# The down products of both feed-forward layers by a seven-product scheme of halves

## The chip, the cores and the metric

The kernel runs on one core of one Trainium2 chip. The metric is device time in microseconds (us) of one execution. A core has TensorE (PE in the profile; PEld is its loading of weights), VectorE (DVE), ScalarE (ACT), GpSimd (POOL) and SyncE (SP), which here only issues DMAs. The engines run their own instruction streams in order and wait for each other by semaphores.

## The reference, cut to what matters

A two-layer trunk over 1024 tokens of width 1024. Layer 0 is a gated mixer, layer 1 an attention over chunks; behind each stands a SwiGLU block, and only that block is changed:

```python
def _swiglu_ffn(x, g_norm, w_gate_up, w_down):     # x: 1024 x 1024
    h = _rms_norm(x, g_norm)
    gate, up = jnp.split(h @ w_gate_up, 2, axis=-1)  # each 1024 x 2816
    return (jax.nn.silu(gate) * up) @ w_down         # w_down: 2816 x 1024
```

Everything is float32, and results have to agree closely with float32.

## The kernel before, in words

All activations stand transposed: features on the 128 partitions, 1024 tokens along the free side. The residual stream x is eight tiles of 128x1024. A float32 number is carried as two parts, hi and lo (`split`, L116: ACT rounds to hi by a copy, DVE takes lo = source - hi), and a product is three matmuls: hi·hi, hi·lo, lo·hi. Every matmul in question is 128x128 weights by 128x512 columns.

A feed-forward block (`ffn`, from L591) has two phases.

*Gate and up*, f = 0 to 21 (a tile of 128 hidden features each, L706). The pair (gate tile f, up tile f) by the pair (token half 1, token half 2) is a 2x2 product of halves, and already done with seven products instead of eight (the Winograd form). Its operands are A (weights; sums S1 to S4 made by POOL, `quad_sum12` and `quad_sum34`) and B (activations; sums T1 to T4 made once). In the steady loop the order on PE is A11·B11, S2·T2, S1·T1, A12·B21, S3·T3, S4·B22, A22·T4, each 12 matmuls, 84 in all. Between them DVE and ACT add up the products, scale by the norm, apply silu (`gate`, L634) and multiply (`up`, L638) into yy, which is stored to memory (`yd`, L755). The weights of f+1 are prepared meanwhile: two loads (`wraw`), four POOL sums, splits of S1|S2, A11|A12, S3|S4 and A22 into four pairs of buffers `whi`, `wlo`, each free once f's product has used it.

*Down*, from L760: 22 K tiles y(f), loaded again from `yd` and split (`load_y`), each with a weight tile `wd` (`prep_w`, L93). Two K tiles at a time, `rows_all` and `mm_rows` (L220) make 8 output tiles times 2 token halves: six matmuls into a PSUM bank, then one DVE addition into x (L230). The last pair of layer 0 goes through `rows_late`, and the last four K tiles of layer 1 too, interleaved with the final norm.

Places in SBUF are few: 28 slots (`slot`) hold B in the first phase and y in the second; eight places (`xplace`) hold x, which in the first phase stands in memory (`xd`), while the places serve as ac, bu, gg and yy of two iterations in turn; three scratch tiles (`scratch`, tag scr) rotate.

The order written in the program is a priority. A planner of the framework, with its own costs, places instructions on each engine's queue and may put a later one that is ready ahead of an earlier one that is not; a new tile waits for all users of the one whose place it takes. All DMAs of these phases are issued by SP, in the planned order.

Of the kernel before, what the change touches and what calls it, by code (L numbers as in the profile page):

```python
# [15 lines left out]
P = 128  # L16
# [33 lines left out]
class Trunk:  # L50
# [492 lines left out]
    QUAD = ("S12", "S34", "A", "AA")  # L543

    def b_plain(self, B, i, xe, xo, ge, go):
# [45 lines left out]
    def ffn(self, x, layer, sqp):  # L591
        nc, a = self.nc, self.a
        with ExitStack() as st:
            psum = self.ps8 if layer == 0 else self.pool(st, "psF", 8, psum=True)
            dp = self.pool(st, f"fdram{layer}", 1, dram=True)
            xd = dp.tile([KT, P, S], F32, name="xd")
            yd = dp.tile([FT, P, S], F32, name="yd")
            self.ffn_slots(st, layer)
            acc = self.const.tile([P, S], F32, name="rbc")
# [3 lines left out]

            def xplace(d, name):
                if layer == 0:
                    return sqp.tile([P, S], F32, name=name, tag=f"x{d}")
                return self.hp.tile([P, S], F32, name=name, tag=f"hhi{d}")

# [21 lines left out]
            def outs(f):  # L630

                return [xplace(4 * (f % 2) + j, f"{n}{f}") for j, n in enumerate(("ac", "bu", "gg", "yy"))]

# [70 lines left out]
            q = qn  # L704
            wl = [(a[f"wd{layer}"][f], None) for f in range(FT)]
            for f in range(2, FT):  # L706
# [43 lines left out]
                up(o, 1, None)  # L750
                self.quad_s34(qn) if more else self.prep_w()
# [3 lines left out]
                nc.sync.dma_start(yd[f], yy)  # L755
                self.quad_a22(qn) if more else self.prep_w()
                q = qn
# [3 lines left out]

            def load_y(f):
                j = 16 + 6 * (f // 2 % 2) + 3 * (f % 2)
# [7 lines left out]
            x = []  # L771
            for d in range(KT):
                x.append(xplace(d, f"x{layer}_{d}"))
                nc.sync.dma_start(x[d], xd[d])
            xt[:] = x
            n = FT if layer == 0 else FT - 4
            for f in range(0, n, 2):
                ws2 = [self.take_w(), self.take_w()]
                ys = [yt.pop(f), yt.pop(f + 1)]
                if layer == 0 and f == FT - 2:  # L780
                    self.rows_late(psum, ws2, ys, x)
                else:
                    self.rows_all(psum, "ps", ws2, ys, x)
                self.prep_w()
                self.prep_w()
                for k in (f + 4, f + 5):
                    if k < FT:
                        load_y(k)
            if layer == 0:
                return x  # L790

            ws4 = [self.take_w() for _ in range(4)]
            ys = [yt.pop(FT - 4 + i) for i in range(4)]
            parts = [slice(0, 512), slice(512, 768), slice(768, 1024)]
            accs, xgs = {}, {}

            def done(d, t):
# [4 lines left out]
                if d < 2:  # L804
                    accs[k] = self.slot(8 + len(accs), f"facc{len(accs)}", F32)[:, 0:w]
                self.square_add(self.hx, accs[k], x[d][:, t], d < 2, eng)
                for c in range(t.start, t.stop, 256):
                    k = (c, d // 4)
                    if d % 4 == 0:
                        xgs[k] = self.slot(len(xgs), f"xg{len(xgs)}", F32).rearrange("p (k t) -> p k t", k=4)  # L810
                    nc.scalar.activation(xgs[k][:, d % 4, :], x[d][:, c:c + 256], AF.Copy,
# [22 lines left out]

            self.rows_late(psum, ws4, ys, x, (parts[0],), done)
            running = [finish(parts[0])]
            for t in parts[1:]:
                for d in range(KT):
                    self.mm_rows(psum, "ps", ws4, ys, x, d, t)
                    done(d, t)  # L840
                    if d in (2, 6):
                        next(running[-1])
# [252 lines left out]
def prepare(i):  # L1095
# [23 lines left out]
    for l in range(2):  # L1119
        gu = i["ffn_w_gate_up"][l]  # L1120
        o[f"wg{l}"] = cols2(gu[:, :FF])
        o[f"wup{l}"] = cols2(gu[:, FF:])
        o[f"wd{l}"] = rows(i["ffn_w_down"][l])
    o["wk"] = cols(i["w_kv"][:, :D])
# [33 lines left out]
```

## Time and profile before

| | |
|---|---|
| median of 3 runs | 2527.73 us (2523.31 to 2528.09) |
| profiled execution | 2528.11 us, its span 2526.3 us |
| granted TensorE clock | 0.995 |
| busy: PE, PEld, DVE | 2466.4, 2041.4, 1710.3 us |
| busy: ACT, POOL | 920.1, 361.8 us |
| DMA | 241.08 MB |
| gate and up, layer 0 and 1 (steady) | about 682 to 1006 and 1942 to 2266 us |
| down, layer 0 and 1 | about 1006 to 1230 and 2266 to 2511 us |

Times in the trace count from the first instruction. "idle before <-releaser" is the time an engine stood still ahead of an instruction and what ended it. Matmuls overlap in the pipeline, so the length of one in the profile is more than the distance from one to the next.

### The profile page before, as it was taken

The page shows a single profiled execution, that of the slowest core. Times are in us where ns is not written, and L with a number is a line of the kernel's source. Part 1 is how long each engine was busy: PE and PEld are TensorE (multiplying, and loading weights), DVE is VectorE, ACT ScalarE, POOL GpSimd, SP SyncE. Part 2 cuts the span into 40 slices and gives each one's busy share as a digit, 9 for nine tenths or more (in the row PEclk, how much of TensorE's full clock was granted, in tenths as well). Part 3 has the DMA queues.
Part 4 walks back from the last instruction along what each step waited for, and adds up shares of the span by engine and source line. Part 5 has one row for each costly group of instructions (what it writes and reads, how often), then busy time and mean ns, then how long its engine had stood idle before and what let it go on. Part 6 is the DMA issues. An engine that isn't in the chain of part 4 may idle for free.

```text
span 2526.3 us, 30361 instructions
## 1 busy us (share of the span) xinstructions
PE 2466.4 (98%) x11646; PEld 2041.4 (81%) x11646; DVE 1710.3 (68%) x2713; ACT 920.1 (36%) x1445; POOL 361.8 (14%) x285
## 2 busy tenths in 40 slices
PE   8999999999999999999999999999999999999997
PEld 6888888887788888888877888877877888888887
DVE  6227677678666566767877777777777656667665
ACT  5123232236333333111445555554453323331113
POOL 3001111121222321000210100000112222210001
PEclk9999999999999999999999999999999999999999
DMA  6223222223222224322322222243322222253222
GB/s 201 83 96 97 67 71 63 67 100 109 92 84 89 79 84 168 141 100 84 127 56 65 65 61 61 66 140 96 128 89 97 79 92 76 83 187 132 91 82 67
DMA packets 94737, 241.08 MB, mean 95 GB/s; under 512 B 8704, under 2 KB 37376, under 8 KB 94592
## 3 DMA queue, kind: packets, MB, share of 16 engines
q1 hardware_dynamic: 92288, 234.95, 28.3%
q10 hardware_dynamic: 2304, 4.20, 0.5%
q8 instruction: 91, 1.49, 0.2%
q14 instruction: 54, 0.44, 0.1%
HBM read 178.29 MB, written 52.43 MB: 91 GB/s over the span
## 4 chain that ended last, share of the span: by engine, by line
PE 86%; DVE 8%; ACT 2%; DMA 2%; issue 1%; POOL 1%; DVEq 0%; SPq 0%; ACTq 0%; POOLq 0%
PE ps L588 29%; PE ps L229 23%; PE pj L215 8%; PE ps L215 7%; PE pj L229 3%; PE po L1005 2%; PE ps L333 2%; PE ps L335 2%; PE ps L334 2%; PE pt L978 2%; PE ps L456 1%; PE s L955 1%; PE s L958 1%; DVE x L459 1%; DVE wlo L118 1%
## 5 line engine op out<-in xcount | busy, mean ns | idle before, releaser
L117 ACT CAST whi<-wraw 128x1024 fp32r<-128x1024 f32 (+1 forms) x213 | 202.1, 962 | 567.4 <-PE ps L229 431.9
L230 DVE TENSOR_TENSOR x<-x,ps 128x512 f32<-128x512 f32 (+1 forms) x432 | 281.4, 674 | 167.4 <-PE ps L229 166.8
L118 DVE TENSOR_TENSOR wlo<-wraw,whi 128x1024 fp32r<-128x1024 f32 (+1 forms) x213 | 235.8, 1117 | 59.4 <-ACT whi L117 59.4
L118 DVE TENSOR_TENSOR wlo<-s,whi 128x1024 fp32r<-128x1024 f32 x84 | 106.7, 1270 | 150.4 <-ACT whi L117 146.0
L117 ACT CAST whi<-s 128x1024 fp32r<-128x1024 f32 x84 | 88.0, 1050 | 320.9 <-POOL s L518 207.5
L517 POOL TENSOR_TENSOR s<-wraw 128x512 f32<-128x512 f32 x42 | 54.5, 1298 | 827.1 <-DMA wraw<-wup 775.8
L588 PE MATMUL ps<-b1h,whi 128*128 128x512 f32 x368 | 144.9, 394 | 7.7 <-ACT whi L117 6.3
L215 PE MATMUL pj<-hhi,whi 128*128 128x512 f32 x368 | 151.3, 411 | 0.2 <-DVE x L459 0.2
L588 PE MATMUL ps<-b1h,wlo 128*128 128x512 f32 x368 | 144.9, 394 | 3.0 <-DVE wlo L118 2.7
L215 PE MATMUL pj<-hlo,whi 128*128 128x512 f32 x368 | 147.6, 401 | 0.0
L215 PE MATMUL pj<-hhi,wlo 128*128 128x512 f32 x368 | 146.6, 399 | 0.0
L588 PE MATMUL ps<-b2h,whi 128*128 128x512 f32 x368 | 143.6, 390 | 1.6 <-ACT ac L681 1.6
L588 PE MATMUL ps<-b1l,whi 128*128 128x512 f32 x368 | 144.4, 392 | 0.0
L588 PE MATMUL ps<-b2l,whi 128*128 128x512 f32 x368 | 143.2, 389 | 0.0
L588 PE MATMUL ps<-b2h,wlo 128*128 128x512 f32 x368 | 143.2, 389 | 0.0
L588 PE MATMUL ps<-bth,wlo 128*128 128x512 f32 x336 | 130.9, 389 | 0.5 <-DVE wlo L118 0.5
L105 POOL TENSOR_TENSOR wraw<-wraw,gv 128x1024 f32<-128x1024 f32 x24 | 48.8, 2038 | 572.4 <-DMA wraw<-wv_att 238.0
L588 PE MATMUL ps<-bth,whi 128*128 128x512 f32 x336 | 130.8, 389 | 0.0
L588 PE MATMUL ps<-btl,whi 128*128 128x512 f32 x336 | 130.7, 389 | 0.0
L396 POOL TENSOR_TENSOR mt<-mt,bbc 128x256 f32<-128x256 f32 x64 | 60.8, 950 | 444.4 <-ACT mt L395 441.5
L967 ACT ACTIVATE p<-p,mn 128x640 f32<-128x640 f32 (+4 forms) x128 | 89.3, 698 | 73.4 <-DVE mn L962 72.1
L117 ACT CAST thi<-pt 128x640 fp32r<-128x640 f32 (+4 forms) x128 | 71.5, 559 | 101.1 <-PE pt L978 100.2
(474 smaller groups left out, 6555.8 us busy)
## 6 DMA issues: line engine op xcount, KB each, us to landing
wraw<-wg SPq DMA_DIRECT2D x44, 512.0 KB, 3.5
wraw<-wup SPq DMA_DIRECT2D x44, 512.0 KB, 3.6
yd<-yy SPq DMA_DIRECT2D x44, 512.0 KB, 3.5
wraw<-wd SPq DMA_DIRECT2D x44, 512.0 KB, 4.4
y<-yd SPq DMA_DIRECT2D x44, 512.0 KB, 5.3
vd<-vt SPq DMA_DIRECT2D x32, 256.0 KB, 2.6
wraw<-wu SPq DMA_DIRECT2D x16, 512.0 KB, 3.6
wraw<-wout SPq DMA_DIRECT2D x16, 512.0 KB, 3.6
```

What stands on the lines that cost most here:

```text
L117: self.nc.scalar.copy(hi, src)
L118: self.nc.vector.tensor_tensor(lo, src, hi.bitcast(F32), ALU.subtract)
L215: nc.tensor.matmul(ps[s], wt[:, c], ht[:, t], start=(kt == 0 and i == 0), stop=(kt == KT - 1 and i == 2),)
L229: nc.tensor.matmul(o, wt[:, c], yt[:, t], start=(j == 0 and i == 0), stop=(j == last and i == 2))
L230: nc.vector.tensor_tensor(x[d][:, t], x[d][:, t], o, ALU.add)
L333: nc.tensor.matmul(ps[tt], hhi[:, t], whi[:, c], start=(kt == 0), stop=False)
L334: nc.tensor.matmul(ps[tt], hhi[:, t], wlo[:, c], start=False, stop=False)
L335: nc.tensor.matmul(ps[tt], hlo[:, t], whi[:, c], start=False, stop=(kt == KT - 1))
L396: nc.gpsimd.tensor_tensor(t2, t2, _bc_mid(bbc[:, g * P:(g + 1) * P], 2), ALU.add)
L517: nc.gpsimd.tensor_tensor(s12[:, HALF[0]], u[:, HALF[0]], u[:, HALF[1]], ALU.add)
L588: nc.tensor.matmul(ps, w[:, c], h, start=(start and i == pairs[0] and n == 0), stop=(stop and i == pairs[-1] and n == 2), skip_group_check ...
L967: nc.scalar.activation(pt[:, 0:nc_], pt[:, 0:nc_], AF.Exp, bias=mn, scale=-1.0, accum_out=sm)
```

## The change

Of the 22 K tiles of each down product, 16 (f = 2 to 17) go through the same seven-product form: four groups g of four K tiles (two halves of two), each with four pairs of output tiles j and j+4. One such step, k = 4g + j, takes the place of 4 K tiles by 2 output tiles by 2 token halves.

Weights come in a new layout `wds`, 128 x (A11|A12|A21|A22) of 256 columns. `down_load` loads a step's tile and a second copy of A22, and POOL makes S1 to S4 in four subtractions or additions of 256 columns; `down_t1` and `down_t2` split 1024 and 768 columns.

The sums T1 to T4 of y are made during gate and up, for two K tiles at a time, by `y_parts`: five pieces of DVE and ACT work, put into the loop by calls of `some()`, three in the next (even) f and two in the one after. Hi and lo parts go to memory (`td`) in seven stores of 512 KB for two K tiles; `load_t` brings them back, 14 tiles for a group. K tiles 0, 1 and 18 to 21 keep the old path. The places of ac, bu and gg are no longer taken in turn, yy goes round three places, and x comes back in another order.

```diff
+    def down_load(self, layer, k):
+        src = self.a[f"wds{layer}"][k]
+        r1 = self.wp.tile([P, 1024], F32, name="wraw", bufs=2)
+        nc.sync.dma_start(r1, src)
+        r2 = self.scratch(f"r2_{k}")
+        nc.sync.dma_start(r2[:, 512:768], src[:, 768:1024])
+        a11, a12, a21, a22 = (r1[:, c:c + 256] for c in (0, 256, 512, 768))
+        TT = nc.gpsimd.tensor_tensor
+        TT(r2[:, 0:256], a11, a21, ALU.subtract)
+        TT(a21, a21, r2[:, 512:768], ALU.add)
+        TT(a22, a21, a11, ALU.subtract)
+        TT(r2[:, 256:512], a12, a22, ALU.subtract)
...
-                return [xplace(4 * (f % 2) + j, f"{n}{f}") for j, n in enumerate(("ac", "bu", "gg", "yy"))]
+                places = (0, 1, 4 if f == 1 else 6, (3, 5, 7)[f % 3])
+                return [xplace(j, f"{n}{f}") for j, n in zip(places, ("ac", "bu", "gg", "yy"))]
+            def y_parts(f):
+                p = (f - 2) // 2
+                ye, yo = ys.pop(f), ys.pop(f + 1)
+                t = self.scratch(f"ty{f}")
+                def out(n, y, place):
+                    hi = xplace(place, f"yh{f}_{n}", F32R)
+                    nc.scalar.copy(hi, y)
+                    lo = y.bitcast(F32R)
+                    TT(lo, y, hi.bitcast(F32), sub)
+                    nc.sync.dma_start(td[p, 2 * n], hi.bitcast(F32))
+                    nc.sync.dma_start(td[p, 2 * n + 1], y)
+                def t12():
+                    TT(t[:, t1], ye[:, t2], ye[:, t1], sub)
+                    TT(t[:, t2], yo[:, t2], t[:, t1], sub)
+                yield t12
+                def t34():
+                    TT(ye[:, t2], yo[:, t2], ye[:, t2], sub)
+                    t4 = xplace(4, f"yt{f}", F32R)
+                    r = t4[:, t2].bitcast(F32)
+                    TT(r, yo[:, t1], t[:, t2], sub)
+                    nc.scalar.copy(t4[:, t1], r)
+                    TT(t4[:, t2], r, t4[:, t1].bitcast(F32), sub)
+                    nc.sync.dma_start(td[p, 6], t4.bitcast(F32))
+                yield t34
+                yield lambda: out(1, yo, 2)
+                yield lambda: out(0, ye, 4)
+                yield lambda: out(2, t, 2)
...
                 self.quad_s12(qn) if more else self.prep_w()
+                some()
                 prod(pa, "A12", "B21")
...
                 self.quad_a(qn) if more else self.prep_w()
+                some()
                 prod(pb, "S3", "T3")
...
+                    d0 = self.down_load(layer, 0)
+                    self.down_t1(d0)
+                some()
                 prod(pb, "A22", "T4", stop=True)
...
+                if f < FT - 4:
+                    ys[f] = yy
+                    if f % 2:
+                        todo += y_parts(f - 1)
+                else:
+                    nc.sync.dma_start(yd[f], yy)
...
-            for f in range(4):
-                load_y(f)
+            load_y(0, 16)
+            load_y(1, 19)
+            order = (2, 4, 5, 7, 6, 0, 1, 3)
+            for d in order:
+                x[d] = xplace(d, f"x{layer}_{d}")
                 nc.sync.dma_start(x[d], xd[d])
...
+            def load_t(g):
+                for n in (0, 4, 2, 6):
+                    for i in range(2):
+                        t = []
+                        for e in range(1 if n == 6 else 2):
+                            t.append(self.slot(14 * (g % 2) + 2 * (n + e) + i, f"t{g}_{n + e}_{i}"))
+                            nc.sync.dma_start(t[-1].bitcast(F32), td[2 * g + i, n + e])
...
+                        yield
+            for _ in load_t(0):
+                pass
+            ws2 = [self.take_w(), self.take_w()]
+            y2 = [yt.pop(0), yt.pop(1)]
+            d1 = self.down_load(layer, 1)
+            for d in order:
+                for s in range(2):
+                    self.mm_rows(psum, "ps", ws2, y2, x, d, HALF[s])
+            def dprod(q, bank_, A, key, into, start=False, stop=False):
+                ahi, alo = q[A]
+                for i in range(2):
+                    c = slice(i * P, (i + 1) * P)
+                    bhi, blo = T[q["g"], key, i]
+                    for n, (w, h) in enumerate(((ahi, bhi), (ahi, blo), (alo, bhi))):
+                        nc.tensor.matmul(q[bank_], w[:, c], h, ...)
+                for d, s in into:
+                    o = x[q["j"] + 4 * d][:, HALF[s]]
+                    TT(o, o, q[bank_], add)
+            for k in range(nq + 1):
+                if k < nq:
+                    qn["B"], qn["C"], qn["A"] = bank(), bank(), bank()
+                q3 = self.down_load(layer, k + 2) if k + 2 < nq else None
+                if q:
+                    dprod(q, "B", "S3", "T3", [(1, 1)])
+                if k < nq:
+                    dprod(qn, "B", "A11", "B11", [(0, 0)], True)
+                    if k:
+                        self.down_t2(qn)
...
+                if q:
+                    dprod(q, "C", "S4", "B22", [(0, 1)], stop=True)
+                if k < nq:
+                    dprod(qn, "C", "S1", "T1", [(1, 1)], True)
+                    dprod(qn, "B", "S2", "T2", [(0, 1)])
+                    if q2:
+                        self.down_t1(q2)
...
+                if q:
+                    dprod(q, "B", "A22", "T4", [(1, 0)], stop=True)
+                if k < nq:
+                    dprod(qn, "A", "A12", "B21", [(0, 0)], True, True)
+                    if g + 1 < ng:
+                        if k % 4 == 0:
+                            loads = load_t(g + 1)
+                        for _ in range(2 + (k % 4 == 0)):
+                            next(loads, None)
+                    else:
+                        f = FT - 4 + k % 4
+                        load_y(f, 3 * (k % 4))
+                q, qn, q2 = qn, q2, q3
```

## Rows read from the trace of the kernel before

**Rows 1.** The page: PE's busy time, and the shares of the ending chain.
```profile
PE 2466.4 (98%) x11646; PEld 2041.4 (81%) x11646; DVE 1710.3 (68%) x2713; ACT 920.1 (36%) x1445; POOL 361.8 (14%) x285
PE 86%; DVE 8%; ACT 2%; DMA 2%; issue 1%; POOL 1%; DVEq 0%; SPq 0%; ACTq 0%; POOLq 0%
```
**Rows 2.** The ending chain in order of time: start, length, what (gate/up, down).
```profile
662.60 343.52 PE ps L588 x1507
1006.12 217.60 PE ps L229 x960
...
1922.70 343.36 PE ps L588 x1507
2266.06 195.84 PE ps L229 x864
```
**Rows 3.** Windows: length; busy of PE, PEld, DVE, ACT, POOL; clock; DMA share; GB/s.
```profile
681.70:1005.80 324.10, 324.10 (x1432) 268.36 (x1431) 196.08 (x257) 105.01 (x139) 81.28 (x64) 1.00 0.28 97
1006.10:1223.70 217.60, 217.60 (x962) 180.18 (x961) 151.84 (x203) 39.09 (x41) 3.75 (x2) 1.00 0.30 105
```
**Rows 4.** DVE groups by line, gate and up of layer 0: busy, mean ns, idle.
```profile
L642 DVE TENSOR_TENSOR yy<-yy,gg 128x512 f32<-128x512 f32 x34 | 23.4, 688 | 0.6
L118 DVE TENSOR_TENSOR wlo<-wraw,whi 128x1024 fp32r<-128x1024 f32 x18 | 21.8, 1210 | 3.1 <-ACT whi L117 3.1
L118 DVE TENSOR_TENSOR wlo<-wraw,whi 128x512 fp32r<-128x512 f32 x17 | 11.5, 679 | 0.0
```
**Rows 5.** DVE and ACT groups by line, down of layer 0 (1050 to 1200).
```profile
L230 DVE TENSOR_TENSOR x<-x,ps 128x512 f32<-128x512 f32 x111 | 73.3, 685 | 46.4 <-PE ps L229 46.4
L118 DVE TENSOR_TENSOR wlo<-wraw,whi 128x1024 fp32r<-128x1024 f32 x14 | 16.5, 1219 | 0.0
...
L117 ACT CAST whi<-wraw 128x1024 fp32r<-128x1024 f32 x13 | 13.1, 1052 | 107.1 <-PE ps L229 107.1
```
**Rows 6.** DVE's order of time, end of f = 19 and most of f = 20.
```profile
969.03 0.68 DVE L118 TENSOR_TENSOR wlo<-wraw,whi 128x512 fp32r<-128x512 f32 x1
...
970.34 0.69 DVE L642 TENSOR_TENSOR yy<-yy,gg 128x512 f32<-128x512 f32 x1
973.58 0.69 DVE L720 TENSOR_TENSOR bu<-ps,ac 128x512 f32<-128x512 f32 x1 [2.55 <-PE ps L588]
978.19 1.34 DVE L118 TENSOR_TENSOR wlo<-s,whi 128x1024 fp32r<-128x1024 f32 x1 [3.91 <-ACT whi L117]
...
981.67 0.69 DVE L729 TENSOR_TENSOR bu<-ps,ac 128x512 f32<-128x512 f32 x1 [0.41 <-PE ps L588]
...
984.39 0.69 DVE L748 TENSOR_TENSOR gg<-ps,bu 128x512 f32<-128x512 f32 x1 [0.57 <-PE ps L588]
```
**Rows 7.** The same f: SP's issue, POOL's sums and ACT's split of S1|S2.
```profile
969.73 0.33 SPq L496 DMA_DIRECT2D wraw<-wup  x1
...
973.30 1.29 POOL L517 TENSOR_TENSOR s<-wraw 128x512 f32<-128x512 f32 x1 [13.68 <-DMA wraw<-wup]
...
975.79 1.28 POOL L518 TENSOR_TENSOR s<-s,wraw 128x512 f32<-128x512 f32 x1
...
977.10 1.05 ACT L117 CAST whi<-s 128x1024 fp32r<-128x1024 f32 x1 [5.72 <-POOL s L518]
```
**Rows 8.** DVE's order of time in f = 21: y0's split ahead of L729.
```profile
1000.04 1.22 DVE L118 TENSOR_TENSOR y0l<-y,y0h 128x1024 fp32r<-128x1024 f32 x1
1001.17 0.68 DVE L729 TENSOR_TENSOR bu<-ps,ac 128x512 f32<-128x512 f32 x1
```
**Rows 9.** POOL and DVE in order of time, where both are at work.
```profile
555.48 1.30 POOL L517 TENSOR_TENSOR s<-wraw 128x512 f32<-128x512 f32 x1 [10.21 <-DMA wraw<-wup]
556.74 2.28 POOL L524 TENSOR_TENSOR s<-wraw 128x512 f32<-128x512 f32 x1
...
593.04 0.74 DVE L577 SCALAR_TENSOR_TENSOR f<-x,gv,f 128x512 f32<-128x512 f32 x1
...
600.21 1.66 POOL L517 TENSOR_TENSOR s<-wraw 128x512 f32<-128x512 f32 x1 [37.61 <-DVE b1l L118]
...
600.65 1.77 DVE L577 SCALAR_TENSOR_TENSOR f<-x,gv,f 128x512 f32<-128x512 f32 x1
```
**Rows 10.** Windows at the change from gate/up to down (columns as in rows 3).
```profile
1000.00:1020.00 20.00, 20.00 (x89) 16.54 (x89) 18.05 (x26) 5.90 (x7) 0.00 (x0) 1.00 0.91 341
```
**Rows 11.** SP's last issues at that change: the store of y21, the last x.
```profile
1012.67 0.32 SPq L755 DMA_DIRECT2D yd<-yy  x1
...
1016.14 0.32 SPq L774 DMA_DIRECT2D x<-xd  x1
```
**Rows 12.** POOL by line: an addition of 256 columns.
```profile
L149 POOL TENSOR_TENSOR facc<-facc,sq 128x256 f32<-128x256 f32 x6 | 4.7, 780 | 18.3 <-ACT sq L148 18.3
```

More of the change, by code (lines that the diff above doesn't have):

```diff
@@ L543, with down_t1, down_t2 @@
     QUAD = ("S12", "S34", "A", "AA")
+    def down_load(self, layer, k):
+        nc = self.nc
+        src = self.a[f"wds{layer}"][k]
[9 more added lines that the diff above has]
+        TT(r2[:, 256:512], a12, a22, ALU.subtract)
+        return {"r1": r1, "r2": r2, "g": k // 4, "j": k % 4}
+    def down_t1(self, q):
+        hi = self.wp.tile([P, 1024], F32R, name="whi", bufs=self.NW)
+        lo = self.wp.tile([P, 1024], F32R, name="wlo", bufs=self.NW)
+        self.split(hi, lo, q.pop("r1"))
+        for i, k in enumerate(("A11", "A12", "S1", "S2")):
+            q[k] = (hi[:, i * 256:(i + 1) * 256], lo[:, i * 256:(i + 1) * 256])
+    def down_t2(self, q):
+        hi = self.wp.tile([P, 1024], F32R, name="whi", bufs=self.NW)
+        lo = self.wp.tile([P, 1024], F32R, name="wlo", bufs=self.NW)
+        self.split(hi[:, 0:768], lo[:, 0:768], q.pop("r2")[:, 0:768])
+        for i, k in enumerate(("S3", "S4", "A22")):
+            q[k] = (hi[:, i * 256:(i + 1) * 256], lo[:, i * 256:(i + 1) * 256])
     def b_plain(self, B, i, xe, xo, ge, go):
@@ L704, in ffn, with some @@
             q = qn
-            wl = [(a[f"wd{layer}"][f], None) for f in range(FT)]
+            wl = [(a[f"wd{layer}"][f], None) for f in (0, 1, FT - 4, FT - 3, FT - 2, FT - 1)]
+            todo = []
+            def some(n=1):
+                for _ in range(n):
+                    if todo:
+                        todo.pop(0)()
             for f in range(2, FT):
@@ L750, in ffn @@
                 up(o, 1, None)
-                self.quad_s34(qn) if more else self.prep_w()
+                if more:
+                    self.quad_s34(qn)
+                else:
+                    d0 = self.down_load(layer, 0)
+                    self.down_t1(d0)
+                some()
                 prod(pb, "A22", "T4", stop=True)
@@ L754, in ffn, with load_y @@
                 up(o, 0, None)
-                nc.sync.dma_start(yd[f], yy)
-                self.quad_a22(qn) if more else self.prep_w()
+                self.quad_a22(qn) if more else self.down_t2(d0)
+                if f < FT - 4:
[4 more added lines that the diff above has]
+                    nc.sync.dma_start(yd[f], yy)
                 q = qn
             yt = {}
-            def load_y(f):
-                j = 16 + 6 * (f // 2 % 2) + 3 * (f % 2)
+            def load_y(f, j):
                 r = self.slot(j, f"y{f}", F32)
@@ L767, in load_y @@
                 self.split(*yt[f], r)
-            for f in range(4):
-                load_y(f)
-            x = []
-            for d in range(KT):
-                x.append(xplace(d, f"x{layer}_{d}"))
-                nc.sync.dma_start(x[d], xd[d])
[L775 to L788, printed above, removed]
@@ L789, in ffn @@
-            if layer == 0:
+            load_y(0, 16)
+            load_y(1, 19)
+            x = [None] * KT
+            order = (2, 4, 5, 7, 6, 0, 1, 3)
+            for d in order:
+                x[d] = xplace(d, f"x{layer}_{d}")
+                nc.sync.dma_start(x[d], xd[d])
+            ng = (FT - 6) // 4
+            T = {}
+            def load_t(g):
[5 more added lines that the diff above has]
+                            nc.sync.dma_start(t[-1].bitcast(F32), td[2 * g + i, n + e])
+                        if n == 6:
+                            T[g, "T4", i] = (t[0][:, t1], t[0][:, t2])
+                        else:
+                            for k, c in zip({0: ("B11", "T3"), 2: ("B21", "B22"), 4: ("T1", "T2")}[n], HALF):
+                                T[g, k, i] = (t[0][:, c], t[1][:, c])
+                        yield
@@ new lines, in ffn @@
+            for _ in load_t(0):
[12 more added lines that the diff above has]
+                    for n, (w, h) in enumerate(((ahi, bhi), (ahi, blo), (alo, bhi))):
+                        nc.tensor.matmul(q[bank_], w[:, c], h, start=(start and i == 0 and n == 0),
+                                         stop=(stop and i == 1 and n == 2), skip_group_check=True)
+                for d, s in into:
+                    o = x[q["j"] + 4 * d][:, HALF[s]]
+                    TT(o, o, q[bank_], add)
@@ L790, in ffn @@
+            self.prep_w()
+            self.prep_w()
+            if layer == 0:
+                for f in (FT - 4, FT - 2):
+                    ws2 = [self.take_w(), self.take_w()]
+                    y2 = [yt.pop(f), yt.pop(f + 1)]
+                    if f == FT - 2:
+                        self.rows_late(psum, ws2, y2, x)
+                    else:
+                        self.rows_all(psum, "ps", ws2, y2, x)
+                    self.prep_w()
+                    self.prep_w()
                 return x
@@ L794, in ffn @@
             ws4 = [self.take_w() for _ in range(4)]
-            ys = [yt.pop(FT - 4 + i) for i in range(4)]
+            ys4 = [yt.pop(FT - 4 + i) for i in range(4)]
             parts = [slice(0, 512), slice(512, 768), slice(768, 1024)]
@@ L1122, in prepare @@
         o[f"wup{l}"] = cols2(gu[:, FF:])
-        o[f"wd{l}"] = rows(i["ffn_w_down"][l])
+        w = o[f"wd{l}"] = rows(i["ffn_w_down"][l])
+        ng = (FT - 6) // 4
+        w = w[2:2 + 4 * ng].reshape(ng, 2, 2, P, 2, 4, P).transpose(0, 5, 3, 4, 2, 1, 6)
+        o[f"wds{l}"] = np.ascontiguousarray(w).reshape(4 * ng, P, 1024)
     o["wk"] = cols(i["w_kv"][:, :D])
```

26 lines of the change are left out of this document (19 added, 7 removed).

## The prediction

> **What bounds the kernel now.** I read the page first: PE is busy for 98% of the span and holds 86% of the chain that ended last [rows 1]. A busy PE need not be a full one, so next came the chain in order of time. There the reader sees four long pieces, gate/up and down of each layer, in which PE runs without a break; the first down piece has 960 matmuls in 217.60 us, 0.2267 us each [rows 2]. The windows by stage say the same: PE busy is as long as the window, at a granted clock of 1.00, which is the higher level, 2.4 GHz [rows 3]. So a matmul taken away there is worth 0.2267 us, as long as whatever is added does not make PE wait. The other engines have room: DVE 61% in gate/up (196.08 of 324.10) and 70% in down, ACT 32% and 18%, POOL 25% and 2%, DMA 0.28 to 0.30 [rows 3].
>
> **What the change removes.** The old form of one step (4 K tiles, 2 output tiles, 2 token halves) is 4 x 2 x 2 x 3 = 48 matmuls; seven products of 2 x 3 are 42. With 16 steps a layer and two layers, 32 x 6 = 192 matmuls go: 192 x 0.2267 = **43.5 us**. All of them stand in the pieces of rows 2, so on the path.
>
> **Down, steady.** A step lasts 42 x 0.2267 = 9.5 us. DVE does 7 additions from PSUM where it did 8, at 0.685 [rows 5], 4.8 us; splits of 1024 columns (1.22, rows 5) and of 768, for which I take 0.95, midway between 512 (0.68) and 1024 (1.21) columns [rows 4]: 7.0 of 9.5 us, 73%. The splits of y leave this phase, but for y18 to y21 in the last group (8.2 of 9.5). The shortest distance between an addition and the product that goes on in its bank is two products, A11 to S2 and S2 to the next S3: 2 x 6 x 0.2267 = 2.7 us, against one split in the way and the addition, 1.2 + 0.7. POOL's four sums of 256 columns are 4 x 0.78 = 3.1 us [rows 12]; ACT's 1.75 tiles at 1.05 [rows 5] are 1.8 us. DMA brings 14 x 0.524 MB per group and 4 x 0.655 MB of weights, 10.0 MB in 38 us, 262 GB/s; the chip moved 341 GB/s over 20 us [rows 10]. All of it hides: 0 us. If that DMA pace fell to the mean of 105 GB/s of rows 3, a group would take 95 us; but that row is a phase that asked for no more. I keep 0, with 0 to 4 us for both layers, since 80% of a pace is close.
>
> **Gate and up.** Two K tiles bring y_parts: t12 is 2 and t34 3 operations of 512 columns at 0.69, the three outs one of 1024 each at 1.21 [rows 4]: 2.1 + 1.4 + 3.6 = 7.1 us of DVE in two f, and 3.5 tiles of ACT at 1.05, 3.7 us. An f lasts 84 x 0.2267 = 19.0 us, so DVE goes from 61% to about 80%. It is not the sum that decides but where it falls. Even f get t12, t34 and one out (4.7 us), odd f two outs (2.4 us). Into the reader's view comes DVE's order in one f [rows 6]: it stands still for 2.55 us ahead of L720 (S2's product) and for 3.91 us ahead of the split of S1|S2. The second gap is a chain: the last split of an f frees `wraw` (969.71), SP issues the next up weights (969.73), they land at 973.3, POOL makes three sums to 977.08, ACT rounds to 978.15, and DVE can split [rows 7]. Behind that split stand gate, the split of A, then L729, which has to empty a bank for A22·T4. L729 ended at 982.36 and S4 before A22·T4 ended by 984.39, where L748 starts [rows 6]: 2.0 us, plus the 0.41 that L729 itself waited, 2.4 us of slack. The new pieces are ready when an f starts. That the planner lets ready later work pass waiting work is seen in f = 21, where y0's split, written behind the whole loop, runs ahead of L729 [rows 8]. So I expect the pieces in the gaps: 2.3 us before POOL starts (971.03 to 973.30) are free, the rest of an even f, 4.7 - 2.3 = 2.4 us, falls beside POOL's sums.
>
> What that costs depends on whether the two run side by side. They do not in two places where both are at work [rows 9]: the second sum takes 2.28 us against 1.30 for the first, and a DVE operation started inside a POOL sum takes 1.77 us where its like beside no sum takes 0.74. The Trainium skill ("SBUF — State Buffer", "SBUF: two separate sides" and "Who interferes with whom") says why: a VectorE instruction with two SBUF inputs and a GpSimd one take turns at a shared port pair, each holding it to its end. Rows 9 agree. By that rule every piece of y_parts beside POOL's sums would push the chain by its whole length.
>
> Taken one after the other, as rows 9 have it, 2.4 us meet 2.4 us of slack, and odd f fit in the first gap. Bounds: 0, if more goes in the first gap or later ones; 4.7 - 2.4 = 2.3 us for two f if none goes in the first gap. There are 16 such pairs: 0 to 37 us. I take 0.4 us for a pair, near the low end because rows 8 show the filling: **+6 us**. Seven stores instead of two for a pair are 5.8 MB with the weights in 38 us, 153 GB/s, under rows 10. Single places for ac, bu and gg cost nothing: ac's last reader (L753) ends before the next A11 product does.
>
> **The change of phase.** Old: the slots were filled by four y tiles, with no wait of PE. New: from about 1001 us, when the B tiles go free, 14 T tiles (7.3 MB), four x tiles that wait for f = 21 (2.1 MB), y21's store (0.5) and the weights of step 1 (0.65) are due, 10.6 MB; at 341 GB/s [rows 10] 31 us, so to 1032. Before, the last x went out at 1016.14, after y21's store at 1012.67 [rows 11]; now it stands behind T tiles. PE has the pair of f = 0, 1 first, 96 x 0.2267 = 21.8 us, to 1027.9. T tiles come in the order of use. Late are the weights of step 1: its first product is due five products on plus one, 1027.9 + 30 x 0.2267 = 1034.7, less 3.1 us of POOL, 1.05 of ACT and 1.2 of DVE = 1029.4; they land at about 1033. That is 4 us a layer, **+8 us** for both. Bounds: 0 (the planner issues them ahead of T) and 13 us a layer (if the pace were 250 GB/s, a quarter lower, the 10.6 MB would end at 1043). Less DVE work there (two splits of y fewer) gains nothing, since PE did not wait.
>
> **Sum.** Against the profiled execution, 2528.1 (span 2526.3 and 1.8 around it): 2528.1 - 43.5 + 6 + 8 = 2498.6; that execution is 0.4 above the median, so **2498 us**.
>
> **Rivals.**
> *All hidden.* The gaps take every piece and step 1's weights go out early: 2527.7 - 43.5 = 2484. For it: rows 2 and 8, and 2.4 us of slack. Against: the DMA sum at the change of phase.
> *The change of phase costs three times as much.* x and T share one queue, DVE's additions into x[3] hold up those of step 0 behind them, and step 1 comes late as well: 12 us a layer with the 6 above, 2484 + 24 + 6 = 2514. For it: 10.6 MB against 21.8 us of cover. Against: the last x is needed only at the end of the first pair, eight banks behind PE.
> *Gate and up loses more than down wins (slower).* Its place is the chain of rows 7: `wup` landing, POOL, ACT, split, L729. A store of 512 KB ahead of `wup` on SP's queue costs 0.524 / 341 = 1.5 us, the alternation with POOL up to 2.4; with the pieces placed behind the split of S1|S2 instead of in its wait, an f's DVE work follows the 8.4 us from 969.71 to 978.15 in one line. At 2 us an f beyond the slack, 32 f give 64 us: 2484 + 8 + 64 = 2556. It turns the sign from (43.5 - 8) / 32 = 1.1 us an f. For it: rows 9, and a chain with 2.4 us of slack in 19. Against: rows 8, and that odd f carry only 2.4 us.
> That the change doesn't do what it says: the matmuls are written out in loops of constant length, so the count can't stay as it is; I give it nothing.
>
> **How the numbers follow.** Forecast 50% (2488 to 2512), all hidden 17%, costly change of phase 14%, slower 19%. 0.2% of the time, 5 us, is about what a measurement of this kernel can tell from no change. Faster than 2522.7: 50 + 17 + 11 (of the third case) = 78%. Within 0.2%: 3 of the third and 5 of the fourth, 8%. Slower: 14%. The range goes from 2483, all hidden, to 2528; above it lies most of the fourth case, below it almost nothing.
>
> **What would show it.** PE has 11646 - 192 = 11454 matmuls. Right: PE without a break in most f, waits of a few us after the pair of f = 0, 1, ended by a weight split of step 1 or an addition into x; down shorter by 21.8 us a layer less that wait. In DVE's order, t12 and t34 stand in the two gaps. Wrong: waits of PE in every f on L729, L722's copy or the S1|S2 split (fourth case); waits in the middle of down on T tiles (my 0 there); POOL's sums as short as before beside DVE's pieces (then rows 9 were misread).

## The result, and the profile after

The changed kernel takes **2555.32 us** (2551.14 to 2560.03, four runs) beside 2525.61 (2523.31 to 2528.09, four runs) of the kernel before: the ratio is 1.0118, interval 1.0093 to 1.0143, so it is slower by about 1.2%. I had forecast 2498, in a range to 2528. The profiled execution has a span of 2558.2 us at a mean granted clock of 0.986; before, the span was 2526.3 at 0.995.

First the page: the busy line (busy, share of the span, instructions), then the shares of the ending chain.

```profile
PE 2453.9 (96%) x11454; PEld 2018.4 (79%) x11454; DVE 1836.8 (72%) x2809; ACT 970.0 (38%) x1509; POOL 500.8 (20%) x413
PE 65%; DVE 17%; DMA 6%; issue 5%; POOL 4%; ACT 3%; SPq 0%; DVEq 0%; POOLq 0%; ACTq 0%
```

The 192 matmuls are gone as announced, 11454 of 11646 [rows 1]. PE's busy time fell by only 12.5 us, though, and its share of the ending chain from 86% to 65%; DVE's rose from 8% to 17%. PE has begun to wait for DVE.

Where in the kernel? The first product on y0 begins layer 0's down phase, and the first on y20 marks its end. The last product on y0 belongs to layer 1: it stands at the end of the first pair of K tiles there, 20.4 us into layer 1's down phase in both kernels (2265.9 to 2286.3 before, 2312.8 to 2333.2 after). The rows are: line, operation, count, duration in ns, first and last start in us.

```profile
L229 PE MATMUL ps<-y0h,whi x32: 389/389/389, 1036.2 to 2333.2; 128*128 128x512 f32 x32
```
```profile
L456 PE MATMUL ps<-y20h,whi x24: 389/389/389, 1238.0 to 2506.0; 128*128 128x512 f32 x24
```

The same starts lay at 1006.0, 2286.3 and 1223.6 before. So the stages changed as follows, in us against the kernel before:

```
stage                                       after
up to down, layer 0             (1006.0)    +30.2
down, layer 0                   (217.6)     -15.8
to layer 1's last product on y0 (1062.7)    +32.5
from there to the end           (240.0)     -15.0
sum                                         +31.9   (the spans: 2558.2 - 2526.3)
```

Down (the second and the fourth stage) won 30.8 of its 43.5 us. Gate and up (the first and the third), for which I had counted 6, lost 62.7. The waits say on what (engine and line that wait, what for, us in total, times, longest):

```profile
PE ps L618 <- DVE bu L804: 41.0, 25, 2.8
PE ps L618 <- ACT ac L791: 7.6, 2, 3.8
PE ps L896 <- ACT whi L117: 4.9, 2, 3.3
```

L804 is the addition that I had followed as L729: it empties a bank of PSUM for A22·T4. It is late 25 times: by 1.6 to 2.5 us in each of the 16 even f from 4 to 18, by 2.8 in f = 19 of each layer, and by 0.2 in seven odd f. The next view is DVE's order of time over the end of one odd f and most of one even f (start, length, line, operation; in brackets the idle time before it and what ended it):

```profile
820.58 1.33 DVE L118 TENSOR_TENSOR wlo<-s,whi 128x1024 fp32r<-128x1024 f32 x1 [6.67 <-ACT whi L117]
...
831.21 0.69 DVE L683 TENSOR_TENSOR ty<-yy 128x512 f32<-128x512 f32 x1
832.86 0.69 DVE L793 TENSOR_TENSOR bu<-ps,ac 128x512 f32<-128x512 f32 x1 [0.97 <-PE ps L618]
833.47 0.68 DVE L684 TENSOR_TENSOR ty<-yy,ty 128x512 f32<-128x512 f32 x1
834.07 1.78 DVE L688 TENSOR_TENSOR yy<-yy,yy 128x512 f32<-128x512 f32 x1
835.78 1.78 DVE L691 TENSOR_TENSOR yt<-yy,ty 128x512 f32<-128x512 f32 x1
837.66 2.13 DVE L678 TENSOR_TENSOR yy<-yy,yh 128x1024 fp32r<-128x1024 f32 x1
839.83 2.20 DVE L118 TENSOR_TENSOR wlo<-s,whi 128x1024 fp32r<-128x1024 f32 x1
841.95 0.68 DVE L693 TENSOR_TENSOR yt<-yt 128x512 fp32r<-128x512 f32 x1
...
843.15 1.21 DVE L678 TENSOR_TENSOR ty<-ty,yh 128x1024 fp32r<-128x1024 f32 x1
844.29 1.21 DVE L118 TENSOR_TENSOR wlo<-wraw,whi 128x1024 fp32r<-128x1024 f32 x1
```

In the odd f DVE stands still for 6.67 us before the split of S1|S2 and does no piece of y_parts there. In the even f it does t12 (L683, L684), t34 (L688, L691, L693), out 1 (the first L678) and out 2 (the second), and soon after L823 out 0 as well. All 7.1 us that I had spread over two f stand in one. Beside them is POOL, for the same f:

```profile
833.70 1.60 POOL L517 TENSOR_TENSOR s<-wraw 128x512 f32<-128x512 f32 x1 [12.87 <-DMA wraw<-wup]
835.27 1.73 POOL L524 TENSOR_TENSOR s<-wraw 128x512 f32<-128x512 f32 x1
836.97 1.74 POOL L518 TENSOR_TENSOR s<-s,wraw 128x512 f32<-128x512 f32 x1
838.78 2.16 POOL L525 TENSOR_TENSOR s<-wraw,s 128x512 f32<-128x512 f32 x1
```

The reader is to see the alternation: DVE's 0.69 becomes 1.78, POOL's 1.29 becomes 1.73, and both go on at one pace of about 1.7 us. The split of S1|S2, which before stood beside no piece, takes 2.20 instead of 1.34 [rows 6]. That chain begins with the issue of the up weights:

```profile
829.99 0.33 SPq L496 DMA_DIRECT2D wraw<-wup  x1
```

The split ends at 842.03, 12.0 us later; before it was 9.8 (969.73 to 979.53, rows 6 and 7). That is 2.2 us late. Then L693 and the split of T1|T2 (841.95 to 842.55 and 843.15 to 844.29 by the starts of what follows, 1.7 us) stand ahead of A's split and L804. Together that is 3.9 us, against the 2.4 of slack that the prediction found. The start of A22·T4 on PE, the product behind L804, shows what comes of it: for the even f before, the odd f and this even f after, then for one f before:

```profile
804.65 0.73 PE L618 MATMUL ps<-bt,whi 128*128 128x512 f32 x2 [2.52 <-DVE bu L804]
...
824.30 0.73 PE L618 MATMUL ps<-bt,whi 128*128 128x512 f32 x2 [0.22 <-DVE bu L804]
...
846.16 0.73 PE L618 MATMUL ps<-bt,whi 128*128 128x512 f32 x2 [2.52 <-DVE bu L804]
```
```profile
965.15 0.61 PE L588 MATMUL ps<-bt,whi 128*128 128x512 f32 x2
```

The up weights of this f also leave late: 5.7 us after the A22·T4 ahead of them begins (829.99 - 824.30), where it was 4.6 (969.73 - 965.15), 1.1 us more. 3.9 + 1.1 - 2.4 = 2.6, and PE waits 2.52. DVE's lag is carried from f to f: in the odd f, which has no piece of its own, the up weights leave 7.3 us after A22·T4 (811.99 - 804.65), 2.8 late, and that alone uses up the slack: 0.22 us of wait.

The longest wait, f = 19, has a cause of its own on top of the lag. There two loads of x and the store of y18 stand ahead of the up weights on SP's queue, and POOL starts 5.6 us after their issue instead of 3.6 [rows 7]; no piece falls in that f:

```profile
979.76 0.42 SPq L496 DMA_DIRECT2D wraw<-wup  x1
```
```profile
985.36 1.30 POOL L517 TENSOR_TENSOR s<-wraw 128x512 f32<-128x512 f32 x1 [19.08 <-DMA wraw<-wup]
```

Some waits cost more than their length. Windows of layer 0's gate and up (columns as in rows 3), the first behind a wait of 1.86 us, the second behind one of 1.96:

```profile
720.00:725.00 5.00, 4.21 (x12) 3.32 (x13) 4.93 (x8) 1.99 (x2) 0.00 (x0) 0.66 0.81 240
762.00:767.00 5.00, 4.30 (x19) 3.53 (x20) 4.93 (x8) 3.16 (x4) 0.00 (x0) 1.00 0.78 245
660.00:1034.00 374.00, 353.38 (x1513) 286.96 (x1512) 286.65 (x338) 136.63 (x178) 100.99 (x70) 0.98 0.42 147
```

In the first stretch the granted clock is 0.66, some of it at the lower level of 1.2 GHz; in the second it stays at 1.00. Such a fall follows eight of the 18 long waits, four in each layer, and costs 1.7 us (0.34 x 5): 6.8 us in layer 0. The stage's mean of 0.98 says the same more coarsely (0.02 x 374 = 7.5). PE's waits there are 20.9 us longer than before (27.7 against 6.8, each summed over the stage). The two make 27.7 of the 30.2 us of layer 0. Over both layers the waits in gate and up are 41.4 us longer (20.9 and 20.5) and the clock takes 13.6: 55.0 of the 62.7.

Down lost 12.7 us, where I had counted 8 for the change of phase. Layer 0, windows at that place, then SP's issue of step 1's weights and PE's wait for their split:

```profile
1045.00:1065.00 20.00, 20.00 (x90) 16.55 (x89) 10.50 (x17) 0.00 (x0) 0.00 (x0) 1.00 0.98 380
1065.00:1085.00 20.00, 16.68 (x67) 13.30 (x66) 13.57 (x16) 4.72 (x5) 13.15 (x15) 0.91 0.95 366
```
```profile
1053.64 1.66 SPq L550 DMA_DIRECT2D wraw<-wds  x2
```
```profile
1068.90 1.91 PE L896 MATMUL ps<-t,whi 128*128 128x512 f32 x4 [3.32 <-ACT whi L117]
```

SP issues step 1's weights at 1053.64, behind the T tiles, 17.4 us after down begins, and PE then waits 3.32 us for their split (1068.90). The clock of 0.91 takes 0.09 x 20 = 1.8 us more. That is 5.1 of the 6.0 us that layer 0 lacks of its 21.8. In layer 1 the same wait is 1.6 us (4.9 in all), of the 6.8 us that it lacks. Another 3.0 us of layer 1 are lost at the very end: the products on y20 beside the final norm take 30.5 us (2512.9 to 2543.4) at a granted clock of 0.89, and took 27.5 (2484.2 to 2511.7) at 1.00 before.

### The profile page after: what moved, and what is told of

Its sections match the earlier page's. It is cut to its first block, busy times and chain, and to the rows that moved or that the text cites. A ratio compares the mean times of both kernels' runs of the same rounds, so it can differ in the third digit from the quotient of the medians.

```text
span 2558.2 us, 30686 instructions
## 1 busy us (share of the span) xinstructions
PE 2453.9 (96%) x11454; PEld 2018.4 (79%) x11454; DVE 1836.8 (72%) x2809; ACT 970.0 (38%) x1509; POOL 500.8 (20%) x413
## 4 chain that ended last, share of the span: by engine, by line
PE 65%; DVE 17%; DMA 6%; issue 5%; POOL 4%; ACT 3%; SPq 0%; DVEq 0%; POOLq 0%; ACTq 0%
PE ps L618 14%; PE ps L896 10%; PE pj L215 8%; PE ps L229 7%; PE ps L215 7%; DVE wlo L118 4%; DMA wraw<-wup 3%; PE pj L229 2%; PE po L1168 2%; PE ps L333 2%; PE ps L335 2%; PE ps L334 2%; PE pt L1141 2%; PE ps L456 1%; PE s L1118 1%
## 5 line engine op out<-in xcount | busy, mean ns | idle before, releaser
L118 DVE TENSOR_TENSOR wlo<-wraw,whi 128x1024 fp32r<-128x1024 f32 (+1 forms) x213 | 239.8, 1130 | 62.7 <-ACT whi L117 62.1
L896 PE MATMUL ps<-t,whi 128*128 128x512 f32 x896 | 278.1, 391 | 6.1 <-ACT whi L117 4.9
L900 DVE TENSOR_TENSOR x<-x,ps 128x512 f32<-128x512 f32 x224 | 151.6, 684 | 74.3 <-PE ps L896 74.2
L896 PEld LDWEIGHTS ps<-t,whi 128*128 128x128 f32 x896 | 168.4, 189 | 43.4 <-ACT whi L117 5.7
L117 ACT CAST whi<-s 128x1024 fp32r<-128x1024 f32 x84 | 88.0, 1050 | 273.2 <-POOL s L518 242.6
L896 PE MATMUL ps<-t,wlo 128*128 128x512 f32 x448 | 174.9, 390 | 0.0
L230 DVE TENSOR_TENSOR x<-x,ps 128x512 f32<-128x512 f32 (+1 forms) x176 | 113.2, 660 | 66.2 <-PE ps L229 62.4
L618 PE MATMUL ps<-bt,whi 128*128 128x512 f32 x336 | 116.8, 431 | 41.7 <-DVE bu L804 41.0
```

What stands on the lines that cost most here:

```text
L117: self.nc.scalar.copy(hi, src)
L118: self.nc.vector.tensor_tensor(lo, src, hi.bitcast(F32), ALU.subtract)
L230: nc.vector.tensor_tensor(x[d][:, t], x[d][:, t], o, ALU.add)
L618: nc.tensor.matmul(ps, w[:, c], h, start=(start and i == pairs[0] and n == 0), stop=(stop and i == pairs[-1] and n == 2), skip_group_check ...
L896: nc.tensor.matmul(q[bank_], w[:, c], h, start=(start and i == 0 and n == 0), stop=(stop and i == 1 and n == 2), skip_group_check=True)
L900: TT(o, o, q[bank_], add)
```

## The experiments

My theory was that gate and up loses by the places of the pieces: so many in the even f, beside POOL and ahead of L804, that the chain from the up weights to L804 outgrows its slack. The rivals: the added work as such (DVE, ACT, stores) is too much; POOL's turns alone do it; or a store ahead of the up weights does it. Each stage is given in us against the kernel before, in the order of the table above.

**The stores without the work.** Sums and hi/lo of y_parts are left out; all seven stores remain.

```diff
...
-                    hi = xplace(place, f"yh{f}_{n}", F32R)
-                    nc.scalar.copy(hi, y)
...
-                    nc.sync.dma_start(td[p, 2 * n], hi.bitcast(F32))
...
+                    nc.sync.dma_start(td[p, 2 * n], y)
...
```

> Leaves out the DVE and ACT work of the pieces (the sums T and the splits of y); their seven stores per pair stay, so the output is not the reference's. Theory (the planner piles the pieces into one f, where they take turns with POOL's sums): the waits of PE on L804's addition go, gate and up fall back to about 344 us a layer, total 2490 to 2500 us. Rival 1 (the stores on SP's queue, or the single places of ac, bu and gg, hold gate and up): little changes, 2540 to 2560 us. Rival 2 (the load of DVE as such): as the theory, 2490 to 2500; this run does not part those two.

Measured: 2498.07 (2489.76 to 2502.92), ratio 0.9891 (0.9862 to 0.992); stages −0.8, −18.3, +2.9, −14.9. The stores by themselves cost gate and up next to nothing (-0.8 + 2.9 = +2.1 us); what costs is the work of the pieces on DVE and ACT, and what it does to POOL. Down keeps most of its loss (43.5 - 33.2 = 10.3 us of 12.7), so that has another cause.

**The pieces without POOL's sums.** All four of each f's sums of weights are left out, S1 to S4 being split from raw weights in their place; the pieces stay.

```diff
...
-                self.quad_s12(qn) if more else self.prep_w()
+                self.quad_split(qn, "S12", ("S1", "S2"), qn["raw"][1]) if more else self.prep_w()
...
-                    self.quad_s34(qn)
+                    self.quad_split(qn, "S34", ("S3", "S4"), qn["raw"][0])
```

> Leaves out POOL's four sums S1 to S4 in the gate/up loop from f = 2 on (the splits read the raw weights instead), so the output is not the reference's; all pieces of y stay. Theory: without POOL at the shared port the pieces take their plain 0.7 and 1.2 us, and the wait for POOL goes, so PE waits for L804 no more than 0.5 us an even f: 2490 to 2510 us. Rival 2 (7.1 us of DVE work more in two f is too much wherever POOL is): waits stay near 1.5 to 2.5 us an even f, 2535 to 2555 us.

Measured: 2482.50 (2478.16 to 2487.03), ratio 0.9833 (0.9808 to 0.9858), below what I expected; stages −7.5, −16.9, −6.5, −16.4. It gains against the kernel before in gate and up too, since the waits for POOL at the start of that loop go as well. DVE's order in an even f:

```profile
811.39 0.69 DVE L688 TENSOR_TENSOR yy<-yy,yy 128x512 f32<-128x512 f32 x1
...
812.79 1.23 DVE L678 TENSOR_TENSOR yy<-yy,yh 128x1024 fp32r<-128x1024 f32 x1
```
```profile
660.00:998.00 338.00, 338.00 (x1491) 279.60 (x1491) 251.87 (x325) 135.05 (x174) 1.77 (x2) 1.00 0.45 162
```

The pieces are piled up as in the changed kernel, but they take their plain durations, and PE runs without a break at a clock of 1.00 (the second fence is a window, columns as in rows 3). So the added work as such is not too much. The run takes away two things at once, though: the turns and the 3.8 us that three of POOL's sums put into the chain [rows 7]. It does not part them.

**No pulling ahead.** Each piece is tied behind the DVE instruction that it is written after.

```diff
-                        todo.pop(0)()
+                        last = next(i for i in reversed(nc.cur_bb.bb.instructions) if i.engine == nc.vector.engine)
+                        with self.tc.issue_after(last):
+                            todo.pop(0)()
```

> Each piece is kept on DVE's queue behind the instruction that stands before it in the program, so that three pieces fall in an even f and two in an odd one, behind the split of S1|S2. Theory: no more turns with POOL's first three sums, but the pieces now stand ahead of L804's addition: by hand it comes 1.0 to 1.5 us late in an even f and up to 0.5 in an odd one, half of what it is now, 2515 to 2540 us. Rival 2: as now, 2550 to 2560 us. Rival 1: as now.

Measured: 2592.96 (2587.93 to 2594.89), ratio 1.0268 (1.0243 to 1.0292): a miss, slower than the change itself; stages +48.8, −18.9, +54.4, −18.1. DVE in an odd f, then SP and POOL of it, then PE's wait on the addition (here L806):

```profile
831.74 1.34 DVE L118 TENSOR_TENSOR wlo<-s,whi 128x1024 fp32r<-128x1024 f32 x1 [8.14 <-ACT whi L117]
833.00 1.21 DVE L678 TENSOR_TENSOR yy<-yy,yh 128x1024 fp32r<-128x1024 f32 x1
...
835.87 1.21 DVE L678 TENSOR_TENSOR ty<-ty,yh 128x1024 fp32r<-128x1024 f32 x1
837.01 0.68 DVE L806 TENSOR_TENSOR bu<-ps,ac 128x512 f32<-128x512 f32 x1
```
```profile
820.60 0.38 SPq L680 DMA_DIRECT2D td<-yy  x1
821.56 0.33 SPq L496 DMA_DIRECT2D wraw<-wup  x1
...
826.84 1.28 POOL L517 TENSOR_TENSOR s<-wraw 128x512 f32<-128x512 f32 x1 [18.51 <-DMA wraw<-wup]
```
```profile
PE ps L618 <- DVE bu L806: 60.7, 18, 4.5
```

The long waits now stand in the odd f, and there are no turns here: POOL's sum takes its plain 1.28. DVE stands still for 8.14 us, and the pieces come after it, where two of them, 2.4 us, are ahead of L806. A store now goes out right ahead of the up weights, and POOL starts 5.3 us after their issue instead of 3.6 [rows 7], 1.7 us late. The issue itself comes 7.2 us after the A22·T4 ahead of it begins (821.56 - 814.33), 2.6 later than the 4.6 before. 2.4 + 1.7 + 2.6 less 2.4 of slack is 4.3; PE waits 3.84 in this f. So the turns are not needed for the loss. Work in the wrong place is enough: what makes the up weights leave late, or stands between their issue and L804, is PE's wait as far as it exceeds the slack.

**The pieces placed by hand.** In even f the four sums go right behind the last multiplication of the f before, ahead of the addition that follows S2's product, and the splits of T4 and of T1|T2 (out 2) behind that addition; in odd f outs 0 and 1 go ahead of it.

```diff
...
-                TT(bu[:, t1], pb, ac[:, t1], add)
+                if todo:
+                    with self.tc.issue_after(last.ins):
+                        todo.pop(0)()
+                bu1 = TT(bu[:, t1], pb, ac[:, t1], add)
+                if todo and f % 2 == 0:
+                    with self.tc.issue_after(bu1.ins):
+                        todo.pop(0)()
...
```

> The pieces are put where DVE stood still before POOL begins: even f, four sums ahead of the addition behind S2 and two splits right behind it; odd f, two splits ahead of that addition. Same work, same stores. Theory: 2.8 and 2.4 us fall in the 2.55 us gap, 1.9 us beside POOL in even f, within the slack of 2.4 us; PE's waits on L804 under 0.5 us an even f, 2490 to 2510 us, faster than the kernel before. Rival 2: 2545 to 2560 us. Rival 1: as now, 2550 to 2560 us.

Measured: 2497.77 (2492.54 to 2507.61), ratio 0.9887 (0.9859 to 0.9914), as expected; stages +3.4, −17.3, +7.5, −14.2. Nothing of the work is left out, and only its places, with the order that follows from them, differ from the changed kernel. DVE in an even f, then PE's wait on the addition (here L813):

```profile
825.21 1.62 DVE L678 TENSOR_TENSOR ty<-ty,yh 128x1024 fp32r<-128x1024 f32 x1
826.75 1.77 DVE L695 TENSOR_TENSOR yt<-yt 128x512 fp32r<-128x512 f32 x1
830.79 1.34 DVE L118 TENSOR_TENSOR wlo<-s,whi 128x1024 fp32r<-128x1024 f32 x1 [2.27 <-ACT whi L117]
...
834.31 0.69 DVE L813 TENSOR_TENSOR bu<-ps,ac 128x512 f32<-128x512 f32 x1
```
```profile
PE ps L618 <- DVE bu L813: 2.5, 5, 0.7
```

Two pieces still take turns with POOL (1.62 and 1.77), yet DVE has 2.27 us left before the split of S1|S2, which is back at 1.34. PE's wait falls from 41.0 us to 2.5.

**Two pieces held back.** The changed kernel with the split of T4 and out 2 behind bu's second addition (here L812), the rest left to the planner.

```diff
...
-                TT(bu[:, t2], pb, ac[:, t1], add)
+                bu2 = TT(bu[:, t2], pb, ac[:, t1], add)
+                if tail:
+                    held[:] = [bu2]
+                    with self.tc.issue_after(bu2.ins):
+                        tail.pop()()
```

> The changed kernel with one thing moved: in an even f the split of T4's sum and the split of T1|T2 (0.7 + 1.2 us of DVE) no longer stand between the split of S1|S2 and L804's addition, but behind that addition. The pieces that take turns with POOL stay. Theory, worked out from the trace of the changed kernel: turns make the split of S1|S2 end 2.2 us later than before, the two splits 1.8 us more, against 2.4 us of slack; without the second part the waits of PE on L804 fall from 41 us to under 15 us in all, and the time to 2505 to 2525 us. Rival: the turns at the port suffice by themselves, waits stay over 25 us, 2535 to 2555 us.

Measured: 2540.65 (2538.37 to 2544.03), ratio 1.0066 (1.0048 to 1.0084), not what I expected of the total; stages +26.6, −17.5, +25.9, −19.2. The waits, and what makes the second:

```profile
PE ps L618 <- DVE bu L812: 18.9, 29, 1.8
PE ps L618 <- ACT ac L803: 16.3, 14, 2.4
```
```profile
810.52 1.05 ACT L677 CAST yh<-yy 128x1024 fp32r<-128x1024 f32 x1 [6.07 <-DMA td<-yt]
```

The wait on the addition is halved, from 41.0 us to 18.9; in most even f it is 0.97 us where it was 1.6 to 2.5. A new wait takes its place: T4's store now goes out later, and ACT's rounding of the next out, which uses the same place (4, of the eight that held x), waits 6.07 us for it. Behind it hang the split that frees `wraw` and with it the issue of the next up weights, 814.06 instead of 811.99 in the changed kernel.

**Step 1's weights ahead of T.** The placed version with one line moved, against the cost of the change of phase.

```diff
+            d1 = self.down_load(layer, 1)
...
-            d1 = self.down_load(layer, 1)
```

> As the placed kernel (2497.8 us), with the load of step 1's weights written ahead of the loads of x and of group 0's T tiles. Theory (step 1's weights stand behind 7 MB of T tiles on SP's queue and come 3 to 4 us late): the wait of PE on the split of step 1's weights goes, from y0's product to the last pair of layer 0 it takes 196 to 198 us instead of 200.3, total 2489 to 2494 us. Rival (those few us lie elsewhere, in x or T tiles that then come later): 2496 to 2500 us.

Measured: 2493.63 (2490.48 to 2496.59), ratio 0.9876 (0.9855 to 0.9897), as expected; stages −0.2, −21.0, +5.9, −17.4. SP's issue, and the window of layer 0's down:

```profile
1000.42 0.33 SPq L550 DMA_DIRECT2D wraw<-wds  x1
```
```profile
1005.80:1202.40 196.60, 196.42 (x865) 161.78 (x864) 142.01 (x188) 40.56 (x44) 57.89 (x63) 1.00 0.63 233
```

The weights leave 5.4 us before down begins instead of 17.4 after, PE is busy for 196.42 of 196.60 us, and the stage gains 21.0 of the possible 21.8. The medians of this run and the placed one are 4.1 us apart with overlapping spreads, and a stage of one trace is no finer: in gate and up, where the two are the same program, the stages differ by 3.6 and 1.6 us. What shows the effect is PE's wait for a split in down, 3.4 us for both layers in the placed version and gone here.

**One place changed.** The version just told, with the copy `ac` of f = 3 in another place, since PE waits 3.8 us for it there.

```diff
-                places = (0, 1, 4 if f == 1 else 6, (3, 5, 7)[f % 3])
+                places = (4 if f == 3 else 0, 1, 4 if f == 1 else 6, (3, 5, 7)[f % 3])
```

> As the run before it, and ac of f = 3 gets place 4 instead of 0, so that its copy need not wait for f = 2's last reader of ac. Theory (the single place of ac costs one wait of 3.8 us a layer, at f = 3, where DVE is behind by the norm's work): that wait falls to 1 us or less, total 3 to 6 us below the run before it. Rival (DVE's lag itself is the limit, L801 or L813 wait in its place): no difference over 1.5 us.

Measured: 2490.92 (2489.57 to 2492.11), ratio 0.9868 (0.9853 to 0.9883); stages +1.4, −21.6, +2.2, −18.1. PE's waits in gate and up:

```profile
PE ps L618 <- DVE bu L813: 4.1, 3, 2.2
...
PE ps L618 <- ACT ac L796: 1.6, 2, 0.8
```

The wait on `ac` goes from 7.5 us to 1.6, and others come up. Against the run before it the gain is 2.7 us, less than I expected, and with overlapping spreads it can't be told from none. Against the kernel before it is the best version that does all the work, 1.3% faster, and 2.5% faster than the change as it was made.

## Why the prediction was wrong

**The removal was right.** 192 matmuls went, and where nothing disturbs down, layer 0's down stage gains 21.0 and 21.6 us (the last two runs) of the 21.8 that 43.5 us for both layers give.

**Down, steady, at nothing: right, within its 0 to 4 us.** In the run with step 1's weights ahead of T, the window 1005.80 to 1202.40 holds the whole of layer 0's stage with 0.2 us of PE idle, at 233 GB/s. In the changed kernel PE waits 1.2 us, both layers together, for additions into x.

**The change of phase, +8 us: right in mechanism and near in size.** The late part was step 1's weights, as the prediction has it. I had put the landing at about 1033 on the old clock, 27 us after down begins; in layer 0 they were issued 17.4 us after it and PE's wait ended 32.7 us after it. The waits are 3.3 and 1.6 us where I had 4 each, and the clock behind the first, which had no term in my sum, is 1.8: 6.7 us. Down lost more, 12.7, because of the 1.2 us just named and of the 3.0 us at the end of layer 1, for which there was no term either. The second is the clock there, 0.89; the kernel before and the version with nothing pulled ahead have 1.00 at that place and take 27.5 us, so the new form does not have to cost it. Why the clock falls there stays open.

**Gate and up, +6 us: this step failed.** It came to 62.7, 3.9 us for a pair of f, where I had 0.4 and an upper bound of 2.3. Four parts of it failed:

- "So I expect the pieces in the gaps": I took the written order, two outs for the odd f, and added that the planner pulls ready work ahead [rows 8]. That fact speaks the other way. In the even f it pulls the odd f's pieces ahead too, 7.1 us instead of 4.7, while the odd f's gap grows to 6.67 us of nothing.
- "2.4 us meet 2.4 us of slack": I counted the pieces beside POOL's sums, but not those behind the split of S1|S2 and ahead of L729. In the trace the turns and longer sums make 2.2 us, L693 and T1|T2 1.7, and the late issue of the up weights 1.1; less 2.4 that is 2.6, and PE's waits in the even f are 1.6 to 2.5. My bound of 2.3 us left the second and third part out. The slack was also read 0.2 us too long: A22·T4 begins at 984.19 in that f, not at 984.39.
- "Single places for ac, bu and gg cost nothing": true of the steady loop, where I looked. At f = 3 of each layer, behind the norm's work, PE waits 3.8 us for the copy of ac, 7.6 in all, for which it did not wait before; the wait is there without the pieces too (7.6 in the first run) and falls to 1.6 with another place (the last).
- No term for the clock: behind eight of the 18 long waits it falls, 6.8 us in each layer.

The price of turns was read rightly from rows 9, 1.77 us for a DVE operation, and 1.78 came. The Trainium skill ("SBUF — State Buffer", "Who interferes with whom") states that a VectorE instruction with two SBUF inputs contends with a GpSimd one that reads SBUF. The trace agrees that the two hold each other up: one of each takes 1.7 us, near the 1.29 + 0.60 = 1.89 of one after the other.

**The rivals.** "Gate and up loses more than down wins" gave 2556, and 2555.32 came, at 19%. Its mechanism was the right one, but that the numbers meet, 62.7 us against its 64, is in part luck: 13.6 of the 62.7 are the clock and 7.6 the copy of ac, which it did not have. Of its three means two acted, the turns with POOL and the pieces behind the split. The third, a store ahead of the up weights, acted in f = 19 alone (5.6 us to POOL's start; in the even f followed above 3.7, before 3.6), and where the stores are tied to their written place. Nor does the loss fall in all 32 f, as the rival had it; PE's waits on L804 stand in the even ones, 34.0 of the 41.0 us, and in f = 19, 5.6.

**Open.** How much of the loss in an even f the turns make by themselves: no run kept the length of POOL's chain and took the turns alone away. The 2.2, 1.7 and 1.1 us are read from one f of the trace; the fifth run, which removed the second part, took 1.5 us off this wait (2.52 to 0.97 in f = 12), which is near the 1.7. That the planner fills one f and leaves the next empty I read from DVE's order alone; why it does so no run shows. Why the clock falls behind some waits and not behind others of the same length stays open too. And 2.5 of the 30.2 us of layer 0 and 5.2 of the 32.5 of layer 1 are not accounted for; part may be the restarts, since a matmul lasts 0.389 us and the next starts 0.2267 after it, by an estimate 0.16 us for each wait beyond its idle time.

## What to carry to other kernels

An engine with a fifth of its time free can still be full at the one place that matters: find the chain with the least slack, here the up weights' issue to L804, and count every added instruction ahead of its end, on each engine that the chain passes. Where a planner may pull ready work ahead, an even load as written is no even load as run; tying the pieces to named instructions turned the same work from 1.2% slower to 1.1% faster. Holding a piece back also holds back its store and the buffer that the store reads, so look for who takes that buffer next.

## What the runs showed of the hardware that was not expected

Behind eight of 18 waits of 1.6 to 2.8 us, in an engine that is busy for 94% of its stage, the granted clock fell, to 0.66 from 720 to 725 us; behind the other ten, 1.6 to 2.5 us long, it did not. In the placed version, with waits of at most 0.7 us on the same addition, it is 1.00 from 660 to 1008 us:

```profile
660.00:1008.00 348.00, 346.67 (x1528) 286.07 (x1527) 274.10 (x340) 138.69 (x180) 101.43 (x72) 1.00 0.46 159
```

A load on SP's queue right behind a store landed some 1.7 us later than one with none ahead of it (5.3 against 3.6 us from issue to POOL's start; 5.6 behind two loads and a store), and with the T tiles the DMA moved 366 to 380 GB/s over 20 us while PE computed, above the 341 that the prediction took as its pace.
